# A prologue that reads x with its rows on partitions, side by side for both halves, in a fused decoder layer

## The chip, the cores and the metric

The kernel runs on one core of a Trainium2 chip. The time is the device time of one execution in microseconds; the median of several executions counts. The engines named below work in parallel, each in its own order: TensorE (PE in the profile) multiplies matrices into PSUM, VectorE (DVE) and ScalarE (ACT) do elementwise work, GpSimd (POOL) does elementwise work on the side, SyncE (SP) issues the DMA transfers.

## The reference

One decoder layer on x of 1024 tokens by 1024 channels, all in float32:

```
c_act = silu(cond);  (sh1, sc1, g1, sh2, ...) = split(c_act @ w_mod + b_mod, 9)
h = rms_norm(x, ffn1_norm) * (1 + sc1) + sh1
x = x + 0.5 * g1 * ((silu(h @ w_gate1) * (h @ w_up1)) @ w_down1)
...                     # conv and S5 mixer from a second modulated norm
x = x + 0.5 * g3 * ((silu(h @ w_gate2) * (h @ w_up2)) @ w_down2)
return rms_norm(x, final_norm)
```

`rms_norm` divides each token's row by the root of its mean square. The gate and up matrices are 1024 by 2816. Only the beginning matters here: the modulation vectors sh1 and sc1, the norm of x, and the first matmuls with h.

## The kernel before, in words

Activations lie transposed: the 1024 channels are eight tiles k of 128 partitions, the 1024 tokens are two halves h of 512 columns. Every f32 value that enters a large matmul is split into a high part in fp32r and a low rest, and `mm3` makes three matmuls of it (high by high, high by low, low by high), each 128 by 512 columns wide. Weights arrive as raw 1 MB tiles (`Weights.load`, at most two in flight) and are split by ACT (high, a cast) and DVE (low, a subtraction) into tiles of a ring with few slots (`pump`, `take`, `free`). w0 and w2 are the first two gate tiles of the feed-forward, w1 and w3 the first two up tiles; the raw tile 0 holds w0 and w1, raw tile 1 w2 and w3.

The prologue (lines 795 to 916) does this: 

- SP loads the bias and gain columns (cols), cond, the first rows of the modulation matrix (mw0, 1 MB), all of x as eight tiles of 0.5 MB with the channels on partitions (`load_x`), the raw weights and the further rows mw1 to mw7. The mw tiles have four buffers, so a later one waits until an earlier one is used up.
- Two f32 matmuls with a row of ones (`cps`) spread cond over all partitions, ACT applies silu: `cact`.
- `mods_of(k)` makes shift and scale of channel tile k by two sweeps of DVE over 1024 columns (a product with `cact` and a sum), and two small operations after them.
- The mean squares: ACT squares each x tile, DVE adds the tiles up, TensorE sums over partitions with matmuls by a column of ones (`p_st`). `roots` computes the inverse roots in nine small DVE operations for both halves at once, `wide` and `spread` bring them back to all partitions by matmuls with the identity (`p0bc`, `p1bc`), ACT copies the result.
- For each k, DVE scales x by the modulation and the root (in place), ACT adds the shift and makes the high part, DVE the low part; then `part(h, k, outs)` issues the matmuls of tile k for output tiles w0 and w1, and for w2 and w3 later. Eight PSUM buffers hold the 2 by 4 sums; 192 matmuls in all.

In the prologue `InOrder.strict` is set: the instructions of DVE, ACT, TensorE and SP then run on their engines in the order in which the program issues them. Instructions given to GpSimd directly (`nc.gpsimd`) are not bound by that. Outside the prologue a scheduler orders the instructions at build time by their dependencies. `Clock` counts calls of `mm3` and hangs side work on them.

After the prologue, `gu_keep` forms silu(gate) * up of the first two output tiles, `gate_up` goes on with the second group (tile names fa1g, fa1u), and `combos1` forms sums and differences of blocks of h, from the scaled x without its shift, which it therefore adds again.

Of the kernel before, what the change touches and what calls it, by code (L numbers as in the profile page):

```python
# [13 lines left out]
F32 = mybir.dt.float32  # L14
# [3 lines left out]
ALU = mybir.AluOpType  # L18
# [23 lines left out]
GB = G // NB  # L42


PAD = 96, 88

C_BMOD, C_N1, C_N2, C_N3, C_NF, C_ONC, C_ONS, C_CW, C_GB = 0, 72, 80, 88, 96, 104, 108, 112, 124
NCOLS = 128
# [184 lines left out]


@with_exitstack
def hymba_layer(ctx: ExitStack, tc, x_d, wm1_d, wmod_d, gu1_d, gs1_d, ds1_d, wl1_d, win_d, wout_d, glu_d, gu2_d, gs2_d, wd2_d, ds2_d, wl2_d, cols_d, cond_d, lam_d, bc_d, out_d):
    nc = tc.nc
    V, A, T, SP = (InOrder(tc, e) for e in (nc.vector, nc.scalar, nc.tensor, nc.sync))

# [29 lines left out]
    def sm(shape, name):  # L269
        return sm_ps.tile(shape, F32, tag="sm", name=name)  # L270
# [144 lines left out]
    def wide(y, nm):  # L415

        q = y.shape[1]
        rb = t2k(nm + "rb")[:, : q * P].rearrange("p (a b) -> p a b", a=q)
        r = V.tensor_scalar(out=rb, in0=y.unsqueeze(2).to_broadcast([P, q, P]), scalar1=0.375, scalar2=None, op0=ALU.mult)
        widened.append(r)  # L420
        return rb

    def spread(rb, nm):
        bc = ps(nm + "bc")
        for i in range(rb.shape[1]):
            T.matmul(bc[:, i * P : (i + 1) * P], lhsT=rb[:, i, :], rhs=ident[:], start=True, stop=True)
        return bc
# [370 lines left out]
    act1 = [[], []]  # L798
    pre = const.tile([P, KT], F32, name="pre")
# [5 lines left out]
    pro = pro_open.enter_context(tc.tile_pool(name="pro", bufs=1))  # L805

    crow = cact[0:1, :]
    InOrder.strict = True
    ones = t2k("ones")[0:1, :P]
    V.memset(ones, 1.0)  # L810
    SP.dma_start(cols[:], cols_d)
    SP.dma_start(crow, cond_d)
    mw = []

    def mod_load(k):
        mw.append(pro.tile([P, 2, 1024], F32, tag="mw", name=f"mw{k}", bufs=4))
        SP.dma_start(mw[k][:], wm1_d[k])

    mod_load(0)
    load_x(range(2))  # L820
    ws.load(1)
    for k in range(1, KT):
        mod_load(k)
        if k == 2:
            ws.load(2)

    b1 = cols[:, C_BMOD + SC1 * KT : C_BMOD + (SC1 + 1) * KT]
    V.scalar_tensor_tensor(out=pre[:], in0=b1, scalar=1.0, in1=cols[:, C_N1 : C_N1 + KT], op0=ALU.add, op1=ALU.mult)
# [4 lines left out]
    for i in range(2):  # L833
        A.activation(cact[:, i * 512 : (i + 1) * 512], cps[i][:], AF.Silu)

    def mods_of(k):

        m = pro.tile([P, 2], F32, tag="m", name=f"m{k}", bufs=2)
        for c in range(2):
            mod_vector(mw[k][:, c, :], m[:, c : c + 1])  # L840
        gn, sh = (cols[:, c + k : c + k + 1] for c in (C_N1, C_BMOD + SH1 * KT))
        V.scalar_tensor_tensor(out=scl[:, 0, k : k + 1], in0=m[:, 0:1], scalar=gn, in1=pre[:, k : k + 1], op0=ALU.mult, op1=ALU.add)
        V.tensor_tensor(out=mods[:, 0, k : k + 1], in0=m[:, 1:2], in1=sh, op=ALU.add)

    mods_of(0)
    st = sm([P, 8], "p_st")
    for h in range(2):
        sqs = []
        for j in range(KT // 2):
            sq = mov(f"p{h}q{j}", dtype=F32)[:].rearrange("p a b -> p (a b)")  # L850
            A.activation(sq, xt[j][h][:].rearrange("p a b -> p (a b)"), AF.Square)
            sqs.append(sq)
            if j:
                V.tensor_tensor(out=sqs[0], in0=sqs[0], in1=sq, op=ALU.add)
        q = sqs[0]
        V.tensor_tensor(out=q[:, :HALF], in0=q[:, :HALF], in1=q[:, HALF:], op=ALU.add)
        for i in range(4):
            c = 4 * h + i
            T.matmul(st[:, c : c + 1], lhsT=q[:, i * P : (i + 1) * P], rhs=one[:], start=True, stop=True)
    y = roots(st, 8, D, "p")  # L860
    rbs = [wide(y[:, 4 * h : 4 * h + 4], f"p{h}") for h in range(2)]
    ws.open(ringp, 2)
    w4 = ws.take(2)
    bcs = []
    for h in range(2):
        bc = spread(rbs[h], f"p{h}")
        bcs.append(pro.tile([P, HALF], F32, tag=f"bc{h}", name=f"bc{h}"))
        A.copy(bcs[h][:], bc[:])
    firsts = [[None] * 4 for h in range(2)]

    def part(h, k, outs):
# [5 lines left out]
    for k in range(KT):  # L877
        for h in range(2):
            V.scalar_tensor_tensor(out=x[k][h], in0=x[k][h], scalar=scl[:, 0, k : k + 1], in1=bcs[h][:], op0=ALU.mult, op1=ALU.mult)
        if k + 1 < KT:  # L880
            mods_of(k + 1)
        sh = mods[:, 0, k : k + 1]
        for h in range(2):
            hi, lo = parts(f"h1{k}_{h}")
            A.activation(hi, x[k][h], AF.Identity, bias=sh)
            V.scalar_tensor_tensor(out=lo, in0=x[k][h], scalar=sh, in1=hi.bitcast(F32), op0=ALU.add, op1=ALU.subtract)
            act1[h].append((hi, lo))
        if k == 1:
            ws.open(ringp, 1)
            ws.open(ring1, 1)  # L890
            w4 += ws.take(2)
        if k < KT - 1:
            for h in range(2):
                part(h, k, (0, 1))
            for j in range(0 if k == 2 else k, k + 1) if k > 1 else ():
                for h in range(2):
                    part(h, j, (2, 3))

    InOrder.strict = False

    def kept_for(g, all_seven=True, split=False):

        return Kept(f"kept{g}", all_seven, split)

    kept = {g: kept_for(g, g not in LAST[0]) for g in range(NGRP)}
    afs = {}
    for fi in range(2):
        for i in (2 * fi, 2 * fi + 1):
            for h in range(2):
                part(h, KT - 1, (i,))  # L910
            ws.free()
        for h in range(2):
            gu_keep(fi, h, firsts[h][2 * fi], firsts[h][2 * fi + 1], afs, kept[0], "fa0")
    ws.retire(ring1)
    pro_open.close()
    ring1_open.close()
# [269 lines left out]

    def combos1():

        sh = mods[:, 0, :]
        both = const.tile([P, 4], F32, name="both")  # L1190
        V.tensor_tensor(out=both[:], in0=sh[:, :4], in1=sh[:, 4:], op=ALU.add)
        blocks.clear()
        blocks.update(A11=act1[0][:4], A12=act1[0][4:], A22=act1[1][4:], S1=[], S2=[], S3=[], S4=[])
        for k in range(4):
            (t11, t21), (t12, t22) = x[k], x[4 + k]
            V.scalar_tensor_tensor(out=t22, in0=t22, scalar=both[:, k : k + 1], in1=t21, op0=ALU.add, op1=ALU.add)
# [5 lines left out]
            V.scalar_tensor_tensor(out=t11, in0=t22, scalar=sh[:, k : k + 1], in1=t11, op0=ALU.subtract, op1=ALU.subtract)  # L1202
            blocks["S2"].append(split_act(t11, f"h1S2_{k}", "B"))
            yield
            V.scalar_tensor_tensor(out=t12, in0=t12, scalar=sh[:, 4 + k : 5 + k], in1=t11, op0=ALU.add, op1=ALU.subtract)
# [502 lines left out]
def _arrays(i):  # L1708
    a = {}
    a["x"] = i["x"].reshape(J, 2, 4, KT, P).transpose(1, 4, 3, 2, 0).reshape(2, P, KT, HALF)  # L1710

    a["wm1"] = i["w_mod"][0].T[: 2 * D].reshape(2, KT, P, D).transpose(1, 2, 0, 3)[:, :, ::-1]
    a["wmod"] = i["w_mod"][0].T.reshape(9, 4, 2, P, 1024).transpose(0, 1, 3, 2, 4)[2:]
    for n in (1, 2):
# [35 lines left out]
    return {k: np.ascontiguousarray(v) for k, v in a.items()}  # L1750


_ORDER = ["x", "wm1", "wmod", "gu1", "gs1", "ds1", "wl1", "win", "wout", "glu", "gu2", "gs2", "wd2", "ds2", "wl2", "cols", "cond", "lam", "bc"]


# [15 lines left out]
```

## Time and profile before

| | us |
|---|---|
| median of 3 runs | 1721.76 |
| lowest, highest | 1721.03, 1724.53 |
| the profiled execution's own time | 1719.28 |
| its span, first to last instruction | 1717.5 |
| TensorE busy | 1657.8 |
| VectorE busy | 1262.0 |
| first matmul with h starts | 29.54 |
| the second group (fa1g) starts | 85.44 |

A row of the timeline gives the start, the time, engine, line, operation, the written and the read tiles, the shape and the count, and in brackets how long the engine was idle before and what ended that. In a row of windows stand the stretch and its length, the busy time and count of PE, PE's weight loads, DVE, ACT and POOL, the granted TensorE clock, and the share and rate of DMA. A group's row ends with its busy time and the mean in ns of one. An f32 matmul appears as two rows in the counts, except for a transpose.

### The profile page before, as it was taken

Reading aid. Unit: us, or ns where it says so; the run is one execution under the profiler, and the core shown is the slowest. Engines: PE = TensorE matmul, PEld = TensorE weight load, DVE = VectorE, ACT = ScalarE, POOL = GpSimd, SP = SyncE. Lnnn points to the kernel's source line nnn. Section 1 sums busy time; section 2 is a strip of 40 time slices with the busy share of each in tenths; the row PEclk is TensorE's granted clock in tenths of the full one; section 3 lists DMA queues with packets and bytes.
Section 4 is the critical chain, followed back from the end, with each engine's and each line's share of the span. In section 5 each row is a group of like instructions: output and inputs, shape, how many; then the busy total and the mean of one; then the engine's idle time right before and its main releaser. Section 6 shows DMA issues by size and latency. Waiting matters only on the chain.

```text
span 1717.5 us, 20689 instructions
## 1 busy us (share of the span) xinstructions
PE 1657.8 (97%) x7484; PEld 1365.9 (80%) x7484; DVE 1262.0 (73%) x1979; ACT 616.0 (36%) x1036; POOL 375.3 (22%) x293
## 2 busy tenths in 40 slices
PE   4999999999999999999999999999999999999997
PEld 3788787888878878787787778888888888888886
DVE  7939798899588997644666977957777667676645
ACT  4225433333364332331113415524434433322233
POOL 0012233223322322100000021132223223333212
PEclk9999999999999999999999999999999999999998
DMA  8222464454564656134655452314444343759212
GB/s 327 78 98 96 148 217 146 160 168 162 199 227 149 233 192 233 70 93 136 207 155 164 135 185 93 128 72 164 183 174 168 147 169 150 268 224 379 109 49 99
DMA packets 101625, 281.48 MB, mean 164 GB/s; under 512 B 19345, under 2 KB 34961, under 8 KB 90386
## 3 DMA queue, kind: packets, MB, share of 16 engines
q1 hardware_dynamic: 101522, 280.15, 46.4%
q8 instruction: 59, 0.97, 0.2%
q14 instruction: 44, 0.36, 0.1%
HBM read 195.69 MB, written 76.02 MB: 158 GB/s over the span
## 4 chain that ended last, share of the span: by engine, by line
PE 50%; DVE 4%; DMA 3%; issue 0%; ACT 0%; SPq 0%; DVEq 0%; ACTq 0%
PE wo L112 4%; PE fb10d L112 2%; PE u L112 2%; PE fbd_1B L112 2%; PE fbd_0B L112 2%; PE b L112 2%; PE v L112 1%; DMA swz<-si 1%; PE fb0u L112 1%; PE fbd_0C L112 1%; PE fbd_1C L112 1%; PE fbd_1A L112 1%; PE fb0d L112 1%; PE fb0g L112 1%; PE fbd_0A L112 1%; PE gl L112 1%
## 5 line engine op out<-in xcount | busy, mean ns | idle before, releaser
L112 ACT CAST w<-raw 128x512 fp32r<-128x512 f32 (+1 forms) x374 | 240.2, 677 | 477.0 <-issue 76.9
L112 DVE TENSOR_TENSOR w<-raw,w 128x512 fp32r<-128x512 f32 (+1 forms) x374 | 309.7, 848 | 114.4 <-ACT w L112 113.6
L177 POOL TENSOR_TENSOR raw<-sums,raw 128x512 f32<-128x512 f32 x54 | 81.4, 1507 | 439.1 <-DVE w L112 426.9
L168 POOL TENSOR_TENSOR sums<-raw 128x512 f32<-128x512 f32 x54 | 75.5, 1398 | 314.0 <-DMA raw<-in_gs 153.7
L179 POOL TENSOR_TENSOR raw<-raw 128x512 f32<-128x512 f32 x54 | 83.2, 1542 | 81.2 <-DVE w L112 81.2
L169 POOL TENSOR_TENSOR raw<-raw 128x512 f32<-128x512 f32 x54 | 85.2, 1578 | 4.2
L112 DVE CUSTOM_DVE_ANT_0 wm<-wm,cact 128x1024 f32<-128x1024 f32 x56 | 77.8, 1401 | 10.1 <-DMA wm<-in_wmod 10.1
L370 POOL TENSOR_TENSOR n3aq<-n3aq,n3aq 128x512 f32<-128x512 f32 x5 | 7.7, 1533 | 276.8 <-ACT n3aq L112 276.6
L112 PE MATMUL p<-h,w 128*128 128x512 f32 x192 | 48.9, 416 | 8.5 <-DVE h L112 5.7
L112 DVE TENSOR_TENSOR w<-sums,w 128x512 fp32r<-128x512 f32 x54 | 53.2, 998 | 2.0 <-ACT w L112 1.4
L112 PEld LDWEIGHTS p<-h,w 128*128 128x128 f32 x192 | 38.5, 202 | 18.7 <-DVE h L112 6.9
L112 PE MATMUL wo<-oa,w 128*128 128x512 f32 x192 | 46.0, 392 | 1.2 <-DVE w L112 0.7
L112 PE MATMUL v<-h,w 128*128 128x512 f32 x192 | 46.9, 395 | 0.0
L112 PE MATMUL c<-h,w 128*128 128x512 f32 x192 | 46.6, 395 | 0.0
L112 PE MATMUL b<-h,w 128*128 128x512 f32 x192 | 45.6, 393 | 0.0
L112 PE MATMUL wo<-ob,w 128*128 128x512 f32 x192 | 45.3, 391 | 0.0
L112 PE MATMUL u<-h,w 128*128 128x512 f32 x192 | 44.7, 392 | 0.2 <-DVE h L112 0.2
L112 ACT CAST w<-sums 128x512 fp32r<-128x512 f32 x54 | 32.8, 620 | 31.0 <-PE fa4gE L112 2.2
L112 PEld LDWEIGHTS wo<-oa,w 128*128 128x128 f32 x192 | 35.7, 188 | 9.6 <-DVE w L112 1.1
L112 PEld LDWEIGHTS u<-h,w 128*128 128x128 f32 x192 | 35.7, 188 | 8.2 <-DVE h L112 0.6
L112 PEld LDWEIGHTS wo<-ob,w 128*128 128x128 f32 x192 | 35.8, 188 | 7.3
L112 PEld LDWEIGHTS b<-h,w 128*128 128x128 f32 x192 | 35.5, 188 | 7.2
(1580 smaller groups left out, 4011.5 us busy)
## 6 DMA issues: line engine op xcount, KB each, us to landing
raw<-in_gs SPq DMA_DIRECT2D x38, 1024.0 KB, 5.2
wm<-in_wmod SPq DMA_DIRECT2D x56, 512.0 KB, 4.8
raw<-in_ds SPq DMA_DIRECT2D x16, 1024.0 KB, 6.7
mw<-in_wm SPq DMA_DIRECT2D x8, 1024.0 KB, 12.7
x<-in_x SPq DMA_DIRECT2D x16, 512.0 KB, 8.3
raw<-in_win SPq DMA_DIRECT2D x8, 1024.0 KB, 5.4
raw<-in_gu SPq DMA_DIRECT2D x6, 1024.0 KB, 10.3
raw<-in_wl SPq DMA_DIRECT2D x5, 1024.0 KB, 6.5
```

Source lines behind the costliest of these rows:

```text
L112: r = getattr(self.engine, name)(*args, **kw)
L168: self.G.tensor_tensor(out=f, in0=r[2], in1=r[1], op=ALU.subtract)
L169: self.G.tensor_tensor(out=r[1], in0=r[1], in1=r[0], op=ALU.subtract)
L177: self.G.tensor_tensor(out=r, in0=s["t3"], in1=r, op=ALU.add)
L179: self.G.tensor_tensor(out=r, in0=self.chunk(j, 3), in1=r, op=ALU.subtract)
L370: nc.gpsimd.tensor_tensor(out=a, in0=a, in1=sq[:, :n], op=ALU.add)
```

## The change

x comes a second time as an input, `xt`: eight blocks of 128 tokens with the tokens on partitions, 128 by 1024 and 0.5 MB each. The prologue loads these instead of `x`, blocks 0 to 3 (half 0) first, before mw0 and the first raw weight tile; then blocks 4 to 7.

- The squares are summed along each row in one operation per block, by `squares` on DVE (blocks 0, 1, 3, 6, 7) or ACT (2, 4, 5), into a column of `st`. No matmuls with ones, no `wide` and `spread`. Each half has its own `roots`, plus one multiplication.
- `scaled` multiplies the rows by their root in place: the columns of k = 0, 1 on ACT, of k = 2, 3 and of k = 4 to 7 on GpSimd, four blocks each.
- `turned` transposes four 128 by 128 pieces to the channel layout in PSUM, one (h, k) at a time, in two buffers; `shifted` lets ACT apply scale and shift from PSUM into x and make the high part; `lows` makes the low part on DVE.
- `mods_of` folds gain, bias and the constant into the two sweeps; its two small operations go. mw has three buffers instead of four.
- `kept_busy` adds matmuls of no use, into a PSUM buffer that nobody reads: four in f32 after `cps`, with block 0 as moving operand, and eight after the first two parts of k = 0. In the counts these are sixteen.
- The order is written out by hand for k = 0 and 1; the outputs of w3 come last for all k, since their PSUM buffers are those of the transposes. The four weight slots are freed together.
- `combos1` finds the shift in x already and uses plain sums. `PAD` and `pre` change so that the other addresses stay.

```diff
@@ prologue
+    def squares(b, engine):
+        if engine is A:
+            A.activation(junks[-1], xb[b], AF.Square, accum_out=st[:, b : b + 1])
+        else:
+            V.tensor_tensor_reduce(out=other, in0=xb[b], in1=xb[b], ..., accum_out=st[:, b : b + 1])
...
+        for c, scale, first, dst in ((0, gn, pre[:, k : k + 1], scl), (1, 1.0, sh, mods)):
+            w = mw[k][:, c, :]
+            V.tensor_tensor_reduce(out=w, in0=w, in1=cact[:], scale=scale, scalar=first, ..., accum_out=dst[:, 0, k : k + 1])
...
+    def root_of(h):
+        y = roots(st[:, 4 * h : 4 * h + 4], 4, D, f"p{h}")
+        V.tensor_scalar(out=root[h], in0=y, scalar1=0.375, scalar2=None, op0=ALU.mult)
+    def scaled(h, lo, hi, engine=A):
+        for b in range(4):
+            part, by = xb[4 * h + b][:, lo * P : hi * P], root[h][:, b : b + 1]
+            if engine is A:
+                A.activation(part, part, AF.Identity, scale=by)
+            else:
+                engine.tensor_scalar(out=part, in0=part, scalar1=by, scalar2=None, op0=ALU.mult)
+    def kept_busy(n, lhsT, rhs):
+        for _ in range(n):
+            T.matmul(filler[:], lhsT=lhsT, rhs=rhs, start=True, stop=True)
+    def turned(h, k):
+        turns[h, k] = sm([P, HALF], f"pt{k}_{h}")
+        for b in range(4):
+            T.transpose(turns[h, k][:, b * P : (b + 1) * P], xb[4 * h + b][:, k * P : (k + 1) * P], ident[:])
+    def shifted(h, k):
+        hi, lo = act1[h][k] = parts(f"h1{k}_{h}")
+        A.activation(x[k][h], turns.pop((h, k))[:], AF.Identity, bias=mods[:, 0, k : k + 1], scale=scl[:, 0, k : k + 1])
+        A.copy(hi, x[k][h])
+    def lows(h, k):
+        hi, lo = act1[h][k]
+        V.tensor_tensor(out=lo, in0=x[k][h], in1=hi.bitcast(F32), op=ALU.subtract)
...
+    squares(0, V); squares(1, V); silu(0); silu(1); squares(2, A); squares(3, V)
+    tok_load(4); mod_load(2); ws.load(2)
+    kept_busy(4, ident[:], xb[0][:, :HALF])
+    root_of(0); scaled(0, 0, 2); scaled(0, 2, 4, nc.gpsimd); mods_of(0); mod_load()
+    turned(0, 0); weight(ringp); shifted(0, 0); lows(0, 0); turned(0, 1)
+    part(0, 0, (0,)); weight(ringp); part(0, 0, (1,))
+    kept_busy(8, w4[0][:, 0, :P], act1[0][0][0])
+    scaled(0, 4, 8, nc.gpsimd)
+    squares(4, A); squares(5, A); squares(6, V); squares(7, V)
+    root_of(1); scaled(1, 0, 2); scaled(1, 2, 4, nc.gpsimd); scaled(1, 4, 8, nc.gpsimd)
+    turned(1, 0); mods_of(1); mod_load(); shifted(1, 0); shifted(0, 1); lows(1, 0); turned(1, 1)
+    part(1, 0, (0, 1)); mods_of(2); mod_load(); lows(0, 1); turned(0, 2); shifted(1, 1)
+    part(0, 1, (0, 1)); weight(ringp); lows(1, 1); turned(1, 2); shifted(0, 2)
+    part(1, 1, (0, 1)); part(0, 0, (2,)); lows(0, 2); mods_of(3); mod_load(); shifted(1, 2); lows(1, 2)
+    part(1, 0, (2,)); part(0, 1, (2,)); part(1, 1, (2,))
+    for k in range(2, KT):
+        if k + 1 < KT: turned(0, k + 1)
+        part(0, k, (0, 1, 2))
+        if k + 1 < KT: turned(1, k + 1); shifted(0, k + 1); shifted(1, k + 1)
+        if k + 2 < KT: mods_of(k + 2)
...
+        if k + 1 < KT: lows(0, k + 1); lows(1, k + 1)
+        if k == 5: weight(ring1)
+        part(1, k, (0, 1, 2))
+    for h in range(2): part(h, 0, (3,))
+    gu_first(0)
+    for k in range(1, KT):
+        for h in range(2): part(h, k, (3,))
```

The lines are set closer here than in the code, where each call has its own line.

More of the change, by code (lines that the diff above doesn't have):

```diff
@@ L797, in hymba_layer @@
     cact = pools["cact"] = cap.tile([P, 1024], F32, name="cact")
-    act1 = [[], []]
-    pre = const.tile([P, KT], F32, name="pre")
+    act1 = [[None] * KT for _ in range(2)]
     ring1_open = ExitStack()
@@ L847, in hymba_layer @@
[L847 to L868, printed above, removed]
+        for c, scale, first, dst in ((0, gn, pre[:, k : k + 1], scl), (1, 1.0, sh, mods)):
+            w = mw[k][:, c, :]
+            V.tensor_tensor_reduce(
+                out=w, in0=w, in1=cact[:], scale=scale, scalar=first, op0=ALU.mult, op1=ALU.add, accum_out=dst[:, 0, k : k + 1]
+            )
@@ L875, in part @@
             mm3(firsts[h][i][:], w4[i], k, act1[h][k], k == 0, k == KT - 1)
-    for k in range(KT):
-        for h in range(2):
[L879 to L897, printed above, removed]
@@ L899, in hymba_layer, with silu @@
-    InOrder.strict = False
[L901 to L913, printed above, removed]
+    def silu(i):
+        A.activation(cact[:, i * 512 : (i + 1) * 512], cps[i][:], AF.Silu)
@@ new lines, in hymba_layer @@
+    scaled(0, 4, 8, nc.gpsimd)
+    squares(4, A)
+    squares(5, A)
+    squares(6, V)
+    squares(7, V)
+    root_of(1)
+    scaled(1, 0, 2)
+    scaled(1, 2, 4, nc.gpsimd)
+    scaled(1, 4, 8, nc.gpsimd)
+    turned(1, 0)
+    mods_of(1)
+    mod_load()
+    shifted(1, 0)
+    shifted(0, 1)
+    lows(1, 0)
+    turned(1, 1)
+    part(1, 0, (0, 1))
+    mods_of(2)
+    mod_load()
+    lows(0, 1)
+    turned(0, 2)
+    shifted(1, 1)
+    part(0, 1, (0, 1))
+    weight(ringp)
+    lows(1, 1)
+    turned(1, 2)
```

133 lines of the change are left out of this document (103 added, 30 removed).

## The prediction

> **What bounds the kernel now.** I read the page's header first, then the windows by stage, then TensorE's timeline.
>
> ```profile
> span 1717.5 us, 20689 instructions
> PE 1657.8 (97%) x7484; PEld 1365.9 (80%) x7484; DVE 1262.0 (73%) x1979; ACT 616.0 (36%) x1036; POOL 375.3 (22%) x293
> ```
> ```profile
> 0.00:45.41 45.41, 19.89 (x61) 13.98 (x62) 33.49 (x62) 20.10 (x23) 0.70 (x6) 0.97 0.82 313
> 45.00:50.00 5.00, 4.59 (x11) 3.63 (x12) 5.00 (x11) 1.39 (x2) 0.00 (x0) 0.52 0.90 321
> 80.00:120.00 40.00, 40.00 (x178) 33.14 (x177) 17.37 (x23) 12.21 (x19) 8.49 (x6) 1.00 0.24 82
> 120.00:160.00 40.00, 40.00 (x177) 32.66 (x176) 32.13 (x66) 15.89 (x29) 6.33 (x37) 1.00 0.26 85
> ```
>
> TensorE (first pair of each row) is idle 59.7 us of 1717.5, and 25.5 of these lie before 45.41. From 80 to 160 it never waits. So time won in the prologue reaches the end, as far as no later stage has its own limit.
>
> ```profile
> 2.91 3.75 PE L112 MATMUL cp<-cact,ones 1*128 1x512 f32 x4 [2.91 <-DMA cact<-in_cond]
> 29.54 0.80 PE L112 MATMUL p<-h,w 128*128 128x512 f32 x1 [1.30 <-ACT h L112]
> 32.86 4.54 PE L112 MATMUL p<-h,w 128*128 128x512 f32 x12 [2.52 <-DVE h L112]
> 38.00 2.83 PE L112 MATMUL p<-h,w 128*128 128x512 f32 x11 [0.60 <-DVE h L112]
> 42.35 0.49 PE L112 MATMUL p<-h,w 128*128 128x512 f32 x1 [1.52 <-ACT h L112]
> 45.41 14.80 PE L112 MATMUL p<-h,w 128*128 128x512 f32 x55 [2.57 <-DVE h L112]
> 79.77 5.83 PE L112 MATMUL p<-h,w 128*128 128x512 f32 x25
> 85.44 11.04 PE L112 MATMUL fa1g<-h,w 128*128 128x512 f32 x48
> 96.32 11.04 PE L112 MATMUL fa1u<-h,w 128*128 128x512 f32 x48
> ```
>
> The first real matmul comes at 29.5, work without a gap from 45.41, and the 192 matmuls of the first group end at **85.44**. That is the number to beat. A warm matmul takes (96.32 - 85.44)/48 = 0.227 us. In between TensorE waits for the activations that DVE and ACT prepare (the idle times in brackets).
>
> **The change, part by part.** Work with x now begins at the first 0.5 MB block, with sums along the row instead of matmuls with ones, and the halves have separate roots. The rows for the walk:
>
> ```profile
> 7.87 1.06 ACT L112 ACTIVATE p0q<-x 128x1024 f32<-128x1024 f32 x1 [0.58 <-DMA x<-in_x]
> 19.37 1.99 ACT L112 CAST w<-raw 128x1024 fp32r<-128x1024 f32 x2 [1.40 <-DMA raw<-in_gu]
> 22.11 0.17 DVE L112 TENSOR_SCALAR pnv<-p_st 128x8 f32<-128x8 f32 x1 [1.96 <-PE p_st L112]
> 23.92 0.43 DVE L112 TENSOR_SCALAR p0rb<-pny 128x512 f32<-128x512 f32 x1
> 24.60 2.35 DVE L112 TENSOR_TENSOR w<-raw,w 128x1024 fp32r<-128x1024 f32 x2
> 34.71 1.22 DVE L112 CUSTOM_DVE_ANT_0 mw<-mw,cact 128x1024 f32<-128x1024 f32 x1
> 35.85 1.22 DVE L112 CUSTOM_DVE_ANT_0 mw<-mw,cact 128x1024 f32<-128x1024 f32 x1
> 41.57 1.39 ACT L112 ACTIVATE h<-x,mods 128x512 fp32r<-128x512 f32 x2 [4.14 <-DVE x L112]
> ```
> ```profile
> L112 ACT ACTIVATE x<-x,cols 128x256 f32<-128x256 f32 x16 | 7.5, 500 | 0.2
> L112 ACT CAST h<-h3t 128x512 fp32r<-128x512 f32 x16 | 9.3, 614 | 0.2
> L112 DVE TENSOR_TENSOR h<-h3t,h 128x512 fp32r<-128x512 f32 x16 | 10.6, 687 | 0.3
> ```
> ```profile
> 256.60 0.66 PE L112 MATMUL tp<-ident,bl 128*128 128x128 f32 x4
> 257.01 2.30 PE L112 MATMUL fa5gD<-h1S,w 128*128 128x512 f32 x9
> ```
>
> *Loads.* The first x tile landed 1.5 MB into the stream at 7.87, the first raw weight 6 MB into it at 19.37: 11.5/4.5 = 2.56 us per MB. In the new order blocks 0 to 3 land at 5.3, 6.6, 7.9, 9.2, modulation rows 0 at 11.7, raw weight 0 at 14.3, blocks 4 to 7 at 15.6 to 19.4, rows 1 and 2 at 22.0 and 24.5, raw weight 1 at 27.1. SP then waits: rows 3 stand behind the last read of rows 0, the third raw weight behind the split of the second tile, later rows behind each sweep. Landing took this long after issue:
>
> ```profile
> DMA to landing us min/median/max: 4.9/12.7/17.1
> ```
>
> Each is issued three sweeps before its use, some 10 us, so I cost them at nothing; without that cover a sweep waits up to 5 us.
>
> *First half.* A sum of squares or one of the two sweeps of mods_of starts 1.15 after the one before (34.71, 35.85). Block 3 is summed at 10.3; nine operations of roots took 23.92 - 22.11 = 1.8, a tenth 0.2: root at 12.4. ACT scales four 256-column pieces at 7.5/16 = 0.47: 14.3; the last transpose 14.5. ACT splits weight tile 0 until 15.3, then shifted: 0.69 (1.39/2) plus 0.58 (9.3/16) = 1.27, to 16.6. DVE does mods_of(0) 12.4 to 14.7, the tile's low part (2.35/2 = 1.18) to 16.5, lows (0.66) to 17.2. The first real matmul is at 16.6 against 29.5; two parts and the second tile are done by 19.
>
> *Second half.* DVE: second tile to 18.8, two sums 21.1, root 23.1. ACT scaling 25.0, shifted(1,0) 26.5, shifted(0,1) 27.7. turned(1,1) needs the PSUM buffer that shifted(0,1) reads, so it runs at 27.3. DVE follows with mods_of(2), lows(0,1), the third tile, lows(1,1): about 32. Eighteen matmuls behind it, and k = 2 starts at **36.0** (all 36 matmuls of k = 0, 1 for three outputs done).
>
> *From there* 156 matmuls at 0.227 and 36 transposes. Four transposes cost 257.01 - 256.60 = 0.41, 0.10 each. 35.4 + 3.7 = 39.1. Per k TensorE needs 18 x 0.227 + 8 x 0.10 = 4.9, DVE 2.3 + 1.3 = 3.6, ACT 4 x 0.6 = 2.5: TensorE is the bound. The end would be 36.0 + 39.1 = **75.1**, a gain of 10.3. Folding scale and shift into the sweep (out of mods_of and combos1) shortens DVE, which is hidden there: nothing. The fourth output's 48 matmuls move behind the loop, and the four weight tiles are given back together: the first is read for the last time 48 x 0.227 = 10.9 before fa1g needs its successor, whose split takes 1.0 + 1.18, so nothing either; without that cover 2.2.
>
> *What speaks against it: GpSimd.* Its 16 scalings run beside DVE's sweeps. No such operation is in this trace; its neighbours are:
>
> ```profile
> L1761 POOL MEMSET const-float32-0.0<- 128x1 f32 x1 | 0.1, 98 | 0.2 <-issue 0.2
> masks.py:197 POOL MEMSET ident<- 128x128 f32 x1 | 0.2, 204 | 0.3 <-POOLq L1761 0.3
> masks.py:199 POOL TENSOR_SCALAR_AFFINE_SELECT ident<-ident 128x128 f32<-128x128 f32 x1 | 0.3, 292 | 0.1
> 1662.35 1.29 POOL L370 TENSOR_TENSOR n_0q<-n_0q,n_0q 128x512 f32<-128x512 f32 x1 [41.60 <-ACT n_0q L112]
> 1673.01 0.74 POOL L370 TENSOR_TENSOR n_0q<-n_0q,n_0q 128x256 f32<-128x256 f32 x1 [3.86 <-ACT n_0q L112]
> 223.85 2.27 POOL L179 TENSOR_TENSOR raw<-raw 128x512 f32<-128x512 f32 x1
> 224.90 2.31 DVE L112 CUSTOM_DVE_ANT_0 wm<-wm,cact 128x1024 f32<-128x1024 f32 x1
> ```
>
> The memsets give 0.8 ns a column (0.52 for 512, 0.31 for 256), the two-operand add 1.29 and 0.74. By the one-operand select, (292 - 98)/127 = 1.5 ns: 0.88 and 0.49; I take these. Each half has four of either: 5.5 us. Side by side the sweep took 2.31 instead of 1.22 and the add 2.27 instead of 1.29: 1.09 lost per 1.29 of GpSimd, 0.84. The scaling reads one operand, not two, so I take half, 0.42 x 5.5 = 2.3 per half, 4.6 in all, less 0.4 that DVE waits there anyway: **4.2**. The bounds are 0 and DVE at 2.31/1.22 throughout (worked out below, 13.7).
>
> The Trainium skill says of this, in "GPSIMD Engine Reference", Specifications, that GpSimd shares its SBUF interfaces with VectorE and contends where a Vector instruction has two SBUF inputs. The trace agrees by the 2.31 against 1.22; without that rule the sum would end at 75.1.
>
> *The useless matmuls.* Four in f32 are eight rows behind cp; a cp row took 3.75/4 = 0.94, so they end by 6.3 + 7.5 = 13.8 at worst, and by about 11 if the clock is granted on the way. The scaling of block 0 must wait until they have read it: 0 to 1.4 after the root at 12.4, and behind it on ACT stand weight tile 0 and shifted(0,0), for which TensorE waits. I take 0, the cp rows being the slow bound. The eight behind part(0,0) end by 19 + 8 x 0.42 = 22.4, before the transposes of half 1 at 25: nothing. Cover gone, they cost what they overrun.
>
> **Sum.** 75.1 + 4.2 = 79.3 against 85.44: a gain of 6.1 us. The profiled execution took 1719.28 (1.8 beyond its span), 2.5 under the median 1721.76; 1719.28 - 6.1 = 1713.2, and from the median **1715.7**.
>
> **The rivals.** *R1, the clock stays low until about 40.* The granted clock fell to 0.50 at 43 after a gap at TensorE, and came back near 49.6, 4.2 us after work resumed at 45.41:
>
> ```profile
> 43.00:44.00 1.00, 0.00 (x0) 0.00 (x0) 1.00 (x3) 0.00 (x0) 0.00 (x0) 0.50 0.40 160
> 49.00:50.00 1.00, 1.00 (x4) 0.81 (x3) 1.00 (x5) 0.00 (x0) 0.00 (x0) 0.59 1.05 442
> ```
>
> At 0.52 a matmul took 4.59/11 = 0.42. From 25 to the start of k = 2 stand 30 matmuls and 20 transposes: 30 x 0.42 + 20 x 0.2 = 16.6, plus some 2 of waiting for the PSUM buffer: 43.6 instead of 40.2. End 82.7, gain 2.7: **1719.0**. For it: TensorE's new stream has waits until 32. Against it: work there is denser than between 29 and 38 before, and the useless matmuls fill two of the gaps. The Trainium skill, "TensorE: Matmul & The Clock Gate", Part 4, says that a transpose in transpose mode does not count as TensorE being busy. By that rule the gaps that transposes fill would still be gaps, which is this rival; the trace has transposes only amid dense matmuls and can't show it.
>
> *R2, slower: GpSimd is the bottleneck.* If a scaling costs as much as the add, 1.29 and 0.74 alone and 1.8 times that in contention, GpSimd works through both stretches. DVE's two-operand work there is 7.6 (a mods_of, two weight splits, a lows, two sums) and 7.8 (two mods_of, a split, three lows); at 2.31/1.22 it grows by 0.89 x 15.4 = 13.7. k = 2 starts at 49.7, the end is 88.8, 3.4 later than before: **1725.2**. It decides once more than 10.3 us are added. For it: the only arithmetic of GpSimd on such tiles in the trace has that price. Against it: that has two operands; select and memset are cheaper per column.
>
> *R3, no change:* what is won is lost again later, at a stage with its own limit (**1721.8**). Against it: TensorE busy 40.00 of 40 in both windows from 80 to 160, DMA at a quarter there.
>
> *R4, GpSimd disturbs nothing:* end 75.1 to 76, **1712.0**. For it, the memset's price; against it, the 2.31.
>
> **How the numbers follow.** Forecast 0.65 (gain 3.5 to 9), R1 0.12, R2 0.08, R3 0.07, R4 0.08. This kernel's runs spread by 0.2%, 3.4 us, so less than that can't be told from no change. Faster is the forecast and R4, 0.73; the same R1 and R3, 0.19; slower R2, 0.08. The range from 1711 (the whole 10.3 and some scatter) to 1721 holds the forecast, R1 and R4 and leaves R2 and R3 out, 0.15.
>
> **What would show it.** Right: fa1g starts near 79 instead of 85.4; the first p matmul near 17 to 18; root of half 0 at 12.4 and of half 1 at 24 to 26; k = 2 near 40 and from there no wait of TensorE; a GpSimd scaling of 0.5 and 0.9, stretched beside DVE, and sweeps of 1.4 to 2 beside it; four transposes in 0.4. R1 shows as a granted clock of 0.5 between 25 and 40, R2 as sweeps over 2 us and TensorE waiting for DVE until 50, R3 as an early fa1g with a later stage that waits longer. A scaling of block 0 that waits for TensorE's useless matmuls would add to every later step. Wrong would be an end of the p matmuls after 82, or one before 75.

## The result, and the profile after

| | before | after |
|---|---|---|
| median of 5 runs each, us | 1721.13 | 1712.95 |
| lowest, highest | 1719.30, 1724.53 | 1711.17, 1714.64 |
| ratio, 95% interval | | 0.9944, 0.9925 to 0.9964 |
| profiled execution | 1719.28 | 1713.61 |
| its span | 1717.5 | 1711.8 |
| the second group (fa1g) starts | 85.44 | 79.79 |

The change makes the kernel faster, by half a per cent. The prediction said 1715.7 and 79.3 for fa1g; fa1g came at 79.79. The two profiled executions differ by 5.67 us at their ends and by 85.44 - 79.79 = 5.65 at fa1g, so in this pair the whole gain is made in the prologue. The medians differ by 8.2; where those 2.5 more may come from is taken up with the last experiments.

The first view of the kernel after is its header and the windows by stage (columns as before: stretch and length, busy time and count of PE, PE's weight loads, DVE, ACT and POOL, the granted clock, DMA share and rate).

```profile
span 1711.8 us, 20820 instructions
PE 1668.0 (97%) x7532; PEld 1369.1 (80%) x7532; DVE 1250.9 (73%) x1957; ACT 624.3 (36%) x1056; POOL 402.7 (24%) x309
```
```profile
0.00:39.99 39.99, 29.50 (x85) 17.77 (x85) 30.60 (x59) 20.28 (x32) 27.27 (x22) 0.87 0.84 343
80.00:120.00 40.00, 40.00 (x178) 33.12 (x177) 12.96 (x18) 8.94 (x15) 6.51 (x5) 1.00 0.21 79
```

TensorE is now idle for 1711.8 - 1668.0 = 43.8 us instead of 59.7, and 10.5 instead of 25.5 of that lie in the prologue. GpSimd, which had 0.70 us of work in the first 45 us, is busy for 27 of the first 40. From 80 on TensorE is full, as before.

TensorE's timeline of the prologue after (start, time, operation, count, and in brackets the idle time ahead of it and what ended it):

```profile
6.19 5.88 PE L112 MATMUL filler<-xb,ident 128*128 128x512 f32 x8
13.87 1.96 PE L112 MATMUL pt<-ident,xb 128*128 128x128 f32 x8 [1.81 <-ACT xb L112]
17.52 3.27 PE L112 MATMUL p<-h,w 128*128 128x512 f32 x6 [1.69 <-ACT h L112]
20.59 2.14 PE L112 MATMUL filler<-h,w 128*128 128x512 f32 x8
25.95 1.52 PE L112 MATMUL pt<-ident,xb 128*128 128x128 f32 x4 [3.21 <-ACT xb L112]
28.34 1.11 PE L112 MATMUL pt<-ident,xb 128*128 128x128 f32 x4 [0.87 <-ACT x L112]
29.11 3.17 PE L112 MATMUL p<-h,w 128*128 128x512 f32 x6
35.43 4.36 PE L112 MATMUL p<-h,w 128*128 128x512 f32 x18
39.99 2.33 PE L112 MATMUL p<-h,w 128*128 128x512 f32 x9
42.16 0.60 PE L112 MATMUL pt<-ident,xb 128*128 128x128 f32 x4
42.51 2.32 PE L112 MATMUL p<-h,w 128*128 128x512 f32 x9
62.67 17.28 PE L112 MATMUL p<-h,w 128*128 128x512 f32 x75
79.79 11.04 PE L112 MATMUL fa1g<-h,w 128*128 128x512 f32 x48
```

The first matmul with h starts at 17.52 instead of 29.54. k = 2 starts at 39.99, for which 40.2 was predicted. The last row with an idle time is that at 28.34: from there to 79.79 TensorE never waits. Nine matmuls and four transposes take 42.51 - 39.99 = 2.52; nine matmuls at 0.227 are 2.04, so the four transposes cost 0.48, 0.12 each, and not 0.10.

The rows of DVE in the same kernel carry the two roots and the sweeps beside GpSimd:

```profile
6.08 1.23 DVE L112 CUSTOM_DVE_ANT_0 junk<-xb 128x1024 f32<-128x1024 f32 x1 [3.00 <-DMA xb<-in_xt]
13.06 0.17 DVE L112 TENSOR_SCALAR py<-p0ny 128x4 f32<-128x4 f32 x1
13.18 1.34 DVE L112 CUSTOM_DVE_ANT_0 mw<-mw,cact,pre 128x1024 f32<-128x1024 f32 x1
14.45 1.49 DVE L112 CUSTOM_DVE_ANT_0 mw<-mw,cact,cols 128x1024 f32<-128x1024 f32 x1
24.89 0.46 DVE L112 TENSOR_SCALAR py<-p1ny 128x4 f32<-128x4 f32 x1
34.66 1.70 DVE L112 TENSOR_TENSOR h<-x,h 128x512 fp32r<-128x512 f32 x2
37.54 1.70 DVE L112 CUSTOM_DVE_ANT_0 mw<-mw,cact,cols 128x1024 f32<-128x1024 f32 x1
```

The root of half 0 is there at 13.23 and that of half 1 at 25.35 (12.4 and 24 to 26 were predicted). The sweeps take 1.34 to 1.70 beside GpSimd. Not all of the growth from the 1.22 of before is GpSimd's: with the gain and the constant folded in, the first sweep of a pair takes 1.34 and the second 1.28 also without GpSimd, as the second experiment shows. And the price of GpSimd itself, from its groups by shape in the first 60 us (busy time and mean ns of one):

```profile
L878 POOL TENSOR_SCALAR xb<-xb,py 128x512 f32<-128x512 f32 x8 | 18.0, 2264 | 0.0
L878 POOL TENSOR_SCALAR xb<-xb,py 128x256 f32<-128x256 f32 x8 | 9.9, 1249 | 12.1 <-DVE py L112 12.1
```

A scaling takes 2.26 us for 512 columns and 1.25 for 256 in the mean, where the prediction took 0.88 and 0.49; the shortest single ones take 1.56 and 0.92. That is close to the price of the slower rival R2, the two-operand add at 1.29 and 0.74 and 1.8 times that beside DVE (2.3 and 1.3). TensorE waits for none of it directly all the same: no row of the timeline names POOL behind "<-".

### The profile page after: what moved, and what is told of

Same layout as the page of the kernel before. It is cut to its first block, busy times and chain, and to the rows that moved or that the text cites. A ratio compares the mean times of both kernels' runs of the same rounds, so it can differ in the third digit from the quotient of the medians.

```text
span 1711.8 us, 20820 instructions
## 1 busy us (share of the span) xinstructions
PE 1668.0 (97%) x7532; PEld 1369.1 (80%) x7532; DVE 1250.9 (73%) x1957; ACT 624.3 (36%) x1056; POOL 402.7 (24%) x309
## 4 chain that ended last, share of the span: by engine, by line
PE 50%; DVE 4%; DMA 3%; issue 0%; ACT 0%; SPq 0%; DVEq 0%; ACTq 0%
PE wo L112 4%; PE fb10d L112 2%; PE u L112 2%; PE fbd_1B L112 2%; PE fbd_0B L112 2%; DMA swz<-si 2%; PE b L112 2%; PE c L112 1%; PE fb0u L112 1%; PE fbd_1C L112 1%; PE fbd_0C L112 1%; PE fbd_1A L112 1%; PE fbd_0A L112 1%; PE fb0d L112 1%; PE fb0g L112 1%; PE v L112 1%
## 5 line engine op out<-in xcount | busy, mean ns | idle before, releaser
L112 PEld LDWEIGHTS b<-h,w 128*128 128x128 f32 x192 | 35.5, 188 | 7.2
```

Source lines behind the costliest of these rows:

```text
L112: r = getattr(self.engine, name)(*args, **kw)
```

## The experiments

The two profiles leave open which part of the change earns the 5.65, what GpSimd costs, and whether the useless matmuls do anything. The starting theory is that of the prediction: half 0's early start earns it, GpSimd takes some back by slowing DVE, and the useless matmuls cost and bring nothing. The rivals: the useless matmuls bring the gain by holding TensorE's clock up; GpSimd costs much more than it seems, because every step behind a root waits for it; only the cheaper operations matter, and the split into halves doesn't.

### Without the useless matmuls

```diff
-    kept_busy(4, ident[:], xb[0][:, :HALF])
     root_of(0)
...
-    kept_busy(8, w4[0][:, 0, :P], act1[0][0][0])
     scaled(0, 4, 8, nc.gpsimd)
```

> The changed kernel without its useless matmuls, early and late. In the changed kernel's trace the granted clock fell to 0.5 at 17.3, just ahead of the first real matmul at 17.5, and again at 27.7, just ahead of the second stretch at 28.3, although the useless matmuls ran at 6.2 to 12.1 and 20.6 to 22.7. Theory A: they change nothing that TensorE's real work sees; fa1g starts at 79.8 give or take 0.4, the time is the changed kernel's within 1 us. Rival B: they hold the clock up; without them it is low for longer behind 34.5 and fa1g starts 1 to 3 us later.

Measured: 1714.93 us against 1723.31 of the kernel before, run beside it, ratio 0.9955 (0.9942 to 0.9968, which overlaps the 0.9925 to 0.9964 of the changed kernel); fa1g starts at 80.01 instead of 79.79. TensorE's timeline of this kernel:

```profile
13.91 2.49 PE L112 MATMUL pt<-ident,xb 128*128 128x128 f32 x8 [7.68 <-ACT xb L112]
17.56 3.27 PE L112 MATMUL p<-h,w 128*128 128x512 f32 x6 [1.17 <-ACT h L112]
29.30 3.11 PE L112 MATMUL p<-h,w 128*128 128x512 f32 x6
```

The sixteen matmuls are worth 0.2 us at fa1g, less than the 0.5 by which fa1g of one and the same changed kernel repeats (last experiment). They do raise the clock: the first eight transposes take 2.49 without them and 1.96 with them. But the first six matmuls with h come at the same time and take 3.27 in both, because the clock has fallen again by then even with them. This is the kernel after (the granted clock is the third number from the end):

```profile
17.00:18.00 1.00, 0.48 (x1) 0.29 (x1) 0.85 (x2) 1.00 (x2) 1.00 (x1) 0.72 1.04 426
18.00:19.00 1.00, 1.00 (x3) 0.61 (x3) 0.79 (x2) 1.00 (x2) 1.00 (x2) 0.50 1.04 434
29.00:34.00 5.00, 5.00 (x16) 3.73 (x15) 5.00 (x7) 4.28 (x7) 5.00 (x4) 0.50 0.87 359
35.00:36.00 1.00, 1.00 (x9) 0.83 (x7) 1.00 (x2) 0.28 (x1) 1.00 (x1) 1.00 1.11 459
```

The second filling of a gap, at 20.59 to 22.73, doesn't prevent the half clock from 28 to 34 either. The rival that the useless matmuls carry the gain is out for this prologue.

One caution on reading that number: in every trace here it stands at 1.00 from the start to the first fall, whatever TensorE does. In the kernel without useless matmuls it shows 1.00 from 14 to 16, beside transposes that take 2.49 instead of 1.96. In the kernel before, it shows 1.00 while the twelve matmuls from 32.86 take 4.54 us, 0.38 each, and the eleven from 38.00 only 0.26 each; their weight loads go from 0.33 to 0.19 near 36. So TensorE ran at about half speed up to 36 in the kernel before, which the 0.97 in the prediction's row does not show. Ahead of the first fall the durations have to tell the clock.

### Without GpSimd

The sixteen scalings on GpSimd are left out, so the channels k = 2 to 7 of x stay without their root; everything else runs as in the changed kernel.

```diff
-    scaled(0, 2, 4, nc.gpsimd)
...
-    scaled(0, 4, 8, nc.gpsimd)
...
-    scaled(1, 2, 4, nc.gpsimd)
-    scaled(1, 4, 8, nc.gpsimd)
```

> The sixteen scalings on GpSimd are left out, so the columns of k = 2 to 7 are not divided by their root; all else stays. Theory A: what GpSimd costs is the stretching of DVE's instructions beside it, which the changed kernel's rows add up to 1.35 before the root of half 1 and 1.7 behind it: sweeps back at 1.22, root of half 1 near 24.0, k = 2 near 37, fa1g at 76.8. Rival B: the predicted price of 4.2, fa1g at 75.6. Rival C: DVE's waits hide it, fa1g at 79 or later.

Measured: 1711.09 us, ratio 0.9929 (0.9910 to 0.9948); fa1g at 78.41, 1.4 earlier than with GpSimd. DVE's and TensorE's rows of this kernel, and a window of it:

```profile
13.15 0.17 DVE L112 TENSOR_SCALAR py<-p0ny 128x4 f32<-128x4 f32 x1
13.27 1.34 DVE L112 CUSTOM_DVE_ANT_0 mw<-mw,cact,pre 128x1024 f32<-128x1024 f32 x1
14.54 1.28 DVE L112 CUSTOM_DVE_ANT_0 mw<-mw,cact,cols 128x1024 f32<-128x1024 f32 x1
23.89 0.17 DVE L112 TENSOR_SCALAR py<-p1ny 128x4 f32<-128x4 f32 x1
32.50 1.48 DVE L112 TENSOR_TENSOR h<-x,h 128x512 fp32r<-128x512 f32 x2
```
```profile
34.05 4.36 PE L112 MATMUL p<-h,w 128*128 128x512 f32 x18
38.61 2.33 PE L112 MATMUL p<-h,w 128*128 128x512 f32 x9
78.41 1.98 PE L112 MATMUL fa1g<-h,w 128*128 128x512 f32 x8
```
```profile
29.00:33.00 4.00, 4.00 (x13) 3.20 (x12) 4.00 (x7) 3.37 (x5) 0.00 (x0) 0.50 1.01 426
```

The last operation of the root of half 1 starts 1.0 earlier and k = 2 starts 1.38 earlier (39.99 - 38.61). So GpSimd's 27.9 us of work cost 1.4 us, not the 4.2 of the prediction and far from 13.7. (Counted from the root of half 0, to take out when x landed, fa1g comes 66.6 and 66.4 us later in the two executions of the changed kernel and 65.1 later here: 1.3 to 1.5.) The result lies between the 76.8 of Theory A and the 79 of Rival C, and the rows say why: DVE's last low parts ahead of k = 2 do start 2.16 earlier (32.50 instead of 34.66), but TensorE, at half clock here too, only comes to its eighteen matmuls at 34.05, 1.38 earlier than the 35.43 of the changed kernel and some 0.8 after the first of these low parts is there. Part of GpSimd's disturbance is thus hidden behind TensorE's slow clock. And without any GpSimd the prologue ends at 78.4, not at 75.1: the rest of the prediction's step-by-step sum was 3.3 too short.

### The wide scalings on ScalarE, and nearly all of them

If GpSimd takes 1.4, ScalarE may take over where it has room. In the first variant the eight 512-column scalings move to ScalarE, in the second the four 256-column ones of half 0 too.

```diff
-    scaled(0, 4, 8, nc.gpsimd)
...
     squares(7, V)
+    scaled(0, 4, 8)
     root_of(1)
...
-    scaled(1, 4, 8, nc.gpsimd)
...
     lows(1, 2)
+    scaled(1, 4, 8)
     part(1, 0, (2,))
```

The second variant adds to this:

```diff
-    scaled(0, 2, 4, nc.gpsimd)
...
+    scaled(0, 2, 4)
     scaled(0, 4, 8)
     root_of(1)
```

> The 512-column scalings (k = 4 to 7) go from GpSimd to ACT: those of half 0 behind its squares, where ACT is idle from 20.7 to 25.4, those of half 1 behind shifted(1,2), where it is idle from 37. GpSimd then works 5 us in each half instead of 28 in all. Theory A (stretching of DVE): the sweeps of mods_of(2) and the split of the third tile go back to 1.22, about half of 3.0 is won, fa1g at 78.3. Rival B (ACT is the next limit): the scaling of half 1 or shifted comes later, fa1g at 79.8 or later.

> As act_wide, and the 256-column scalings of half 0 go to ACT too, into the same idle stretch; only those of half 1 stay on GpSimd. Theory A: the first mods_of and the first weight splits lose their stretching as well, two thirds of 3.0 are won, fa1g at 77.6. Rival B: ACT has 4.4 us to fit into 4.7, the scaling of half 1 starts later than DVE's root, fa1g at 79 or later.

Measured: fa1g at 78.08 with the wide ones on ScalarE and at 77.21 with nearly all. The times: 1714.93 us, ratio 0.9948 (0.9934 to 0.9962), and 1715.03 us, ratio 0.9954 (0.9941 to 0.9967). GpSimd's row of the second variant:

```profile
L878 POOL TENSOR_SCALAR xb<-xb,py 128x256 f32<-128x256 f32 x4 | 5.3, 1347 | 22.1 <-DVE py L112 22.1
```

Both come out at fa1g near what Theory A said (78.3 and 77.6), and the last is 2.6 us ahead of the changed kernel there (0.7 of that from block 3, whose sum ended that much earlier in this execution). They don't split GpSimd's cost any finer: counted from the root of half 0, fa1g comes 64.6 and 64.7 us later, somewhat sooner than the 65.1 with no scaling on GpSimd at all. The clock has a hand in that: it is at 0.50 from about 28.6 to 32 and from 26.8 to 30.2 in these two executions, half as long as without GpSimd. The medians of the whole kernel don't show the earlier fa1g; the last experiments return to that.

### Useless matmuls in the prologue of before

In the kernel before, the clock fell to 0.50 ahead of 45.41. Sixteen useless matmuls in that gap say what such matmuls can be worth.

```diff
+    filler = ps("filler")
...
+            if k == 1:
+                for _ in range(16):
+                    T.matmul(filler[:], lhsT=w4[0][:, 0, :P], rhs=act1[0][0][0], start=True, stop=True)
```

> The kernel before, with sixteen useless matmuls behind the parts of k = 1, in the gap from 40.8 to 45.4, and nothing else. Theory A: the clock, which fell to 0.5 at 43 and rose near 49.6, stays at 1.0; the ten matmuls that ran at 0.42 run at 0.23, fa1g starts at 83.4 instead of 85.4, 2 us less. Rival B: the gap left over is enough for the clock to fall, fa1g stays at 85.4.

Measured: 1718.82 us (12 runs) against 1721.95 (28 runs), ratio 0.9981 (0.9970 to 0.9992); fa1g at 83.23 instead of 85.44. TensorE's timeline of it:

```profile
40.50 3.79 PE L112 MATMUL filler<-h,w 128*128 128x512 f32 x16
45.25 38.15 PE L112 MATMUL p<-h,w 128*128 128x512 f32 x167 [0.73 <-DVE h L112]
83.23 3.11 PE L112 MATMUL fa1g<-h,w 128*128 128x512 f32 x13
```

The work with h resumes at 45.25 at the full clock (167 matmuls in 38.15, 0.228 each) and saves 2.2 us of the 85.44. So useless matmuls paid where a long stretch without waiting followed at once and would have begun at half clock. In the new prologue the stretch at half clock from 28 to 34 comes after a wait of 3.21 ahead of 25.95 that they don't reach; filling that gap too was not tried.

### Transposes instead of the first useless matmuls

```diff
-    kept_busy(4, ident[:], xb[0][:, :HALF])
+    for _ in range(30):
+        T.transpose(filler[:, :P], xb[0][:, :P], ident[:])
```

> The four early useless matmuls of the changed kernel are replaced by thirty transposes of the same block into the same buffer. In the changed kernel the rows of the useless matmuls shrink from 0.85 to 0.43 near 10.4, so the clock rose there. Theory A (the Trainium skill, TensorE: Matmul & The Clock Gate, Part 4: transposes do not count as busy): the thirty stay at about 0.2 each to their end near 12.2. Rival B: they count, and go from about 0.2 to 0.1 near 10.4, so that the last ends by 11.4. By both fa1g stays at 79.8 within 0.5, since the scaling waits for the root at 13.2.

Measured: 1716.93 us, ratio 0.9968 (0.9950 to 0.9987); fa1g at 78.86, outside the 79.8 within 0.5, but with its first root 0.75 earlier (the first operation of the root at 10.52 instead of 11.27), since x landed earlier. What matters here is TensorE's weight loads, since the granted clock shows 1.00 from the start up to 14 (one load of these takes 0.14 up to then, and 0.23 behind the fall of the clock in the window from 14 to 15):

```profile
6.05 5.72 PEld L112 LDWEIGHTS filler<-ident,xb 128*128 128x128 f32 x30 [1.50 <-issue]
13.12 0.14 PEld L112 LDWEIGHTS pt<-ident,xb 128*128 128x128 f32 x1 [1.34 <-ACT xb L112]
16.76 0.29 PEld L112 LDWEIGHTS p<-h,w 128*128 128x128 f32 x1 [1.70 <-ACT h L112]
```

Within the thirty, the load goes from 0.23 to 0.14 near 11, after some 5 us of transposes and the matmuls of cp ahead of them, and the first transposes of x load at 0.14, as fast as behind the useless matmuls. The thirty end at 12.0, near the 12.2 of Theory A, but only because the rise came near 11 and not near 10.4. Without either kind of filling, with the same matmuls of cp, the transposes of x load at 0.18 to 0.23. In this kernel, then, transposes do raise the clock; whether they would without the matmuls of cp just ahead was not tried. The Trainium skill says otherwise, in "TensorE: Matmul & The Clock Gate", Part 4, for the transpose mode; by these rows the measurement decides, for f32 transposes of 128 by 128 as this kernel issues them. By 16.76 the clock is down again here too (0.50 granted from 15 to 18).

### One start for both halves

The squares of blocks 4 to 7 are put ahead of the root of half 0, so half 0 starts only when all of x is there.

```diff
     kept_busy(4, ident[:], xb[0][:, :HALF])
+    squares(4, A)
+    squares(5, A)
+    squares(6, V)
+    squares(7, V)
     root_of(0)
...
-    squares(4, A)
-    squares(5, A)
-    squares(6, V)
-    squares(7, V)
     root_of(1)
```

> The squares of blocks 4 to 7 go ahead of the root of half 0, so that no half starts before all of x has landed. Theory A (a chain: the root of half 1 sets what follows, and DVE's work for half 0 hides the landing of half 1): half 0 starts 10 us later, the root of half 1 comes near 31.5 instead of 25.3, k = 2 near 46, fa1g at 86: the whole gain is gone. Rival B (DVE's total work sets k = 2, in whatever order): only the idle time until block 7 lands is lost, fa1g at 83.

Measured: 1720.57 us (10 runs), ratio 0.9988 (0.9975 to 1.0001); fa1g at 87.03, 7.2 later than in the changed kernel and 1.0 later than Theory A said. TensorE's timeline:

```profile
23.13 2.52 PE L112 MATMUL pt<-ident,xb 128*128 128x128 f32 x8 [10.78 <-ACT xb L112]
26.78 3.27 PE L112 MATMUL p<-h,w 128*128 128x512 f32 x6 [1.12 <-ACT h L112]
41.68 0.33 PE L112 MATMUL pt<-ident,xb 128*128 128x128 f32 x1 [1.00 <-POOL xb L878]
42.58 0.33 PE L112 MATMUL pt<-ident,xb 128*128 128x128 f32 x1 [0.57 <-POOL xb L878]
87.03 1.30 PE L112 MATMUL fa1g<-h,w 128*128 128x512 f32 x5
```

Without the early start of half 0 nothing is left of the gain at fa1g: with all the cheaper operations of the change but a common start, it lies 1.6 behind the kernel before. Here GpSimd does hold TensorE up, 1.57 us, because its scalings begin only behind the late root; without that wait fa1g would come near 85.5, level with before (an estimate, 87.03 - 1.57). In the changed kernel they are hidden, as half 0's can start at 13.4. The order of the rest stayed as it was made for two halves; one made for a common start was not tried. Over the whole time the 1.6 does not show: the interval of the ratio, 0.9975 to 1.0001, leaves at most 0.2 us of it, so something behind fa1g gives it back here. What, was not followed up.

### The same kernels once more

The median of the changed kernel lay 8.2 us under that of before, the prologues 5.65 apart; and act_nearly_all gains 2.6 more at fa1g that its median doesn't show. So the two kernels and that variant ran again, each with a profile of its own.

> The kernel before, unchanged, run as if it were a changed one, with its own profile. Question: the runs of one kernel lie some 3 to 6 us apart, and the spans of the profiles so far differ by more than their prologues do. Theory S: the rest is a varying number of short stretches at the half clock (some 3.4 us each, 1.7 us lost), which the granted clock of 20 us windows behind the prologue shows: in the first profile of before 3.6 us lost in two places (480-500 and 920-940). It expects the ratio at 1.000 within 0.002, the prologue's end (first fa1g matmul) again at 85.4 within 0.4, other places of the lost clock, and span less lost clock again at 1714 within 1. Theory T: the later stages differ by the build's order of the instructions, fixed for a kernel: then the same two places show the same loss, and the span comes out at 1717.5 whatever the clock did elsewhere.

> The changed kernel, unchanged, once more, beside the kernel before of the same call. Theory S (scatter from stretches at the half clock, the gain from the prologue alone): fa1g again at 79.8 within 0.4; span less the clock lost behind the prologue again at 1708 within 1, and below that of the kernel before by 5.0 to 6.5; ratio 0.9967 (5.65 of 1721) plus what the number of such stretches adds or takes, 0.995 to 0.998. Theory T (the new order of the later stages is worth another 2 to 3 us, as the first comparison's 8.2 to 9.6 us would have it): ratio 0.9944 to 0.9952 again, and the stretch from fa1g to the end less its lost clock shorter than that of the kernel before by 2 to 3.

> The variant with twelve of the sixteen GpSimd scalings on ScalarE, once more, beside the changed kernel and the kernel before of the same call. Its fa1g came 2.6 earlier than the changed kernel's, yet its median was no better in its first comparison. Theory S: fa1g again at 77.2 within 0.4, span less lost clock 2 to 3 below that of the changed kernel; the medians differ by 2.6 less or more what the stretches at the half clock do (so -5 to +1). If the rest were fixed by the build (T), the median comes out level with the changed kernel's, within 1, although fa1g is 2.6 earlier, and the stretch from fa1g to the end less its lost clock is 2 to 3 longer.

| | median, us (runs) | ratio, 95% interval | fa1g | span |
|---|---|---|---|---|
| before_again | 1721.05 (11) | 0.9993, 0.9981 to 1.0006 | 85.87 | 1720.5 |
| after_again | 1714.15 (6) | 0.9959, 0.9943 to 0.9975 | 79.30 | 1709.2 |
| nearly_all_again | 1713.31 (9) | 0.9955, 0.9941 to 0.9969 | 77.91 | 1707.0 |

fa1g repeats within 0.7 us. The spans don't: the same kernel before took 1717.5 and 1720.5. One place shows why. First the kernel before in its first profile (timeline and windows), then in its second:

```profile
186.76 2.97 PE L112 MATMUL fa3gC<-h1S,w 128*128 128x512 f32 x12 [2.28 <-DVE fa3gt L112]
```
```profile
186.00:191.00 5.00, 4.24 (x19) 3.56 (x20) 5.00 (x6) 2.78 (x5) 4.48 (x3) 1.00 0.23 52
```
```profile
187.41 4.46 PE L112 MATMUL fa3gC<-h1S,w 128*128 128x512 f32 x12 [2.31 <-DVE fa3gt L112]
```
```profile
186.00:191.00 5.00, 3.59 (x9) 2.89 (x10) 4.51 (x6) 3.14 (x6) 3.64 (x3) 0.66 0.30 78
```

The same wait of 2.3 us stands ahead of the same twelve matmuls. Behind it the clock stays at 1.00 in one execution and falls in the other, and the twelve take 4.46 instead of 2.97. The kernel after has that fall at this place as well (fa3gC x12 in 4.57), and it is not of its making: in all twelve traces of this case the wait here is 2.28 to 2.32, and the fall comes in six of them. The Trainium skill has a mechanism for this, in "TensorE: Matmul & The Clock Gate", Part 1: the activity that sets the clock is counted in windows that run freely, whatever the kernel does, so the outcome depends on where a wait falls in them. The two rows fit that; the page's figure of about 3.4 us of idling for a fall does not fit, since a wait of 2.3 was enough here.

Over windows of 20 us from 60 to 1700, the time lost to the lower clock is 3.6 us in the first profile of before (480 to 500 and 920 to 940) and 5.4 in the second (180, 720 and 960). So the stretches are not fixed to the kernel, which decides for the first of the two theories on the places. Its numbers it meets only in part: the medians came as it said, but fa1g missed its bounds of 0.4 narrowly in two runs and by 0.3 in the third, and span less lost clock is 1715.1 for before_again and 1705.6 for after_again, 9.5 apart and not 5.0 to 6.5. The stretch from fa1g to the end less the lost clock was 1628.5, 1629.2 and 1624.9 in the three executions with the prologue of before (two of before and before_useless, mean 1627.5), and 1626.2 to 1629.3, mean 1627.9, in the nine with the new one. These means show no gain behind fa1g; but single executions scatter there by 4 us, for which I have no cause beyond the clock, and so few of them would not show 2 us. The repeat's interval, 0.9943 to 0.9975, is a gain of 4.3 to 9.8 us, which holds the prologue's 5.65; that of the first comparison, 6.2 to 12.9 us, does not. So the prologue's 5.65 is shown, and whether another 1 or 2 us come behind it stays open.

The variant with nearly all scalings on ScalarE is ahead of the changed kernel by 1.4 to 2.6 at fa1g, and its median by 0.8 in the repeat. Its span less lost clock is 1704.2, 1.4 below the changed kernel's and not 2 to 3; and 2.8 us of lost clock are taken off for the last window alone, 1680 to 1700, in which the clock falls earlier than in the other executions. Without that window the figure is 1707.0, 1.4 above, and its stretch from fa1g to the end 2.8 longer, as Theory T would have it. So this pair does not decide between the two theories. The intervals of the two ratios overlap almost wholly, so that it is the better kernel is shown for the prologue and not for the whole time.

## Why the prediction was right, and where it wasn't

The direction, the place and the size were right: 79.3 predicted for fa1g, 79.79 and 79.30 measured; k = 2 at 40.2 predicted, 39.99 measured. The mechanism was right too: an early start of half 0 that nothing behind it takes back. But the closeness of the number is luck: two errors cancel.

- **GpSimd's disturbance**, the one term charged against the change, was put at 4.2 and measured 1.4 (fa1g 79.79 against 78.41 without it). Both factors failed, in opposite directions. The prices 0.88 and 0.49, read from a select of 128 columns, were too low by 2.6 times (2.26 and 1.25), and by some 1.8 times against even the shortest scalings (1.56 and 0.92): the nearest row was a different operation of a quarter of the width. The disturbance, put at 0.42 us per us of GpSimd, is 1.4/27.9 = 0.05 at the end of the chain, and 2.16 in the 21.3 us up to 34.66, 0.10, at DVE's last low parts, before TensorE's half clock hides a part. Beside the scalings DVE's sweeps grow from 1.34 and 1.28 to at most 1.62 and 1.70, not to 2.31; the row of 2.31 is beside a two-operand add.
- **The sum without GpSimd**, 75.1, was 3.3 too short (78.41). Roots: 13.3 and 24.1 instead of 12.4 and 23.1, 0.9 late from the start; block 3 landed at about 10.0 and not at 9.2 (DVE waits for it), and each sum needs a short operation behind it that reads its result. From the second root to k = 2: 14.6 instead of 12.9, 1.7 more. About 0.8 of that is TensorE at half clock, which the sum had at full clock; 0.35 are the transposes of the next tile, which run ahead of k = 2; the rest are smaller things, such as sweeps of 1.34 and 1.28 and an activation with shift of 0.78 and not 0.69. From k = 2 to fa1g: 39.8 instead of 39.1, from transposes at 0.12 and not 0.10.
- **The first half** showed as predicted: the first matmul with h at 17.52, in the 17 to 18 given.
- **The useless matmuls**, costed at nothing: at most 0.2 us of use at fa1g. Right, and not for want of an effect on the clock, but because the clock is down again before the first matmul that counts.
- **R1**, the clock low until 40, happened in part: 0.50 from 28 to 34, then full. It cost little, since the first of DVE's last two low parts ahead of k = 2, begun at 34.66, is there only at about 35.5, when TensorE has got there at half clock (35.43); the two were level. Without GpSimd the half clock was the later of the two.
- **R2**, GpSimd the bottleneck: its condition, a scaling as dear as the add and 1.8 times that in contention (2.3 and 1.3), was met closely (2.26 and 1.25), but its second factor, DVE slowed by 1.9, was not. In the kernel with a common start GpSimd did reach TensorE, 1.57 us.
- **R3**, the gain lost behind the prologue, did not happen in the changed kernel. **R4**, GpSimd disturbs nothing, was nearly right on the disturbance and wrong on the time it gave, by the 3.3 of that sum.
- The base in the text was the median 1721.76; with 5.65 measured at fa1g it gives 1716.1. The medians 1712.95 and 1714.15 lie lower by 2 to 3 us, within the scatter of the stretches at half clock.

## What to carry to other kernels

When a prologue waits for all of its input before the first matrix product, split the input so that one half can begin: here nothing of the gain was left without that start, and the cheaper operations alone, in an order made for two halves, were worth none. Before matmuls of no use are added to hold a clock, look at whether the stretch that they warm runs on without a wait; ahead of a long one they were worth 2.2 us here, between short ones 0.2 at most. And a total that comes out right proves no term of its sum: take out the disputed term by itself.

## What the runs showed of the hardware

- GpSimd scales 128 by 512 f32 by a per-row factor in 2.26 us and 128 by 256 in 1.25 (1.35 and 1.38 in the variants with fewer of them, 1.89 and 1.57 for the two widths in the kernel with a common start; single ones from 1.56 and 0.92 up), all of it in stretches where DVE works too; its own two-operand add of 128 by 512 took 1.29 in one row and 2.27 beside a sweep. How long it takes with an idle DVE was not measured.
- Thirty f32 transposes in a row, about 0.20 us each, right behind the matmuls of cp, brought TensorE's clock to full near 11 us.
- The granted clock reads 1.00 in these traces up to the first fall, also where matmuls take 0.38 instead of 0.23 to 0.26 us.
- A wait of 2.3 us ahead of the same matmuls lets the clock fall in six of twelve traces, at 1.5 us a time (4.46 against 2.97). With the few such places of this kernel it is a part of why its runs lie 3 to 6 us apart.
